# Two of eleven row-tile pairs in two feed-forward out projections computed as seven block products

## The chip, the cores and the metric

The kernel runs on one core of one Trainium2 chip. The metric is the device time of one execution in microseconds, the median of the runs. A profile comes from one execution more, whose own time is given beside it. Engines are named as in the profile: PE multiplies matrices, DVE and ACT and POOL work on tiles, SP issues the transfers.

## What is computed

A decoder trunk of two layers on 256 tokens of width 1024. Each layer wraps its mixer (a short gated convolution in the first layer, sparse attention in the second) in two half-step feed-forward blocks, so four such blocks run one after the other, each with an in projection (1024 to 5632) and an out projection (2816 to 1024). All data is float32.

```python
D_MODEL, SEQ, DEPTH, N_A_LAYERS, D_FF = 1024, 256, 2, 1, 2816

def swiglu_ffn(x, w_in, w_out):
    gate, up = jnp.split(x @ w_in, 2, axis=-1)
    return (jax.nn.silu(gate) * up) @ w_out

for i in range(DEPTH):
    if i == N_A_LAYERS:
        kv = shared_kv(h, ...)
    h = h + 0.5 * swiglu_ffn(rmsnorm(h, ffn1_norm[i]), ffn1_w_in[i], ffn1_w_out[i])
    hn = rmsnorm(h, mix_norm[i])
    if i < N_A_LAYERS:
        h = h + short_conv_mixer(hn, conv_w_in[i], conv_w[i], conv_w_out[i])
    else:
        h = h + nsa_mixer(hn, ...)
    h = h + 0.5 * swiglu_ffn(rmsnorm(h, ffn2_norm[i]), ffn2_w_in[i], ffn2_w_out[i])
```

The change concerns the two out projections of the first layer (i = 0): `ffn1_w_out[0]`, which stands before the convolution, and `ffn2_w_out[0]`, which stands before the shared K/V projection and the second layer.

## The kernel before

**Split products.** Every float32 operand is split in two fp32r tiles: `high`, a cast, and `low`, the float32 value less that cast. A product of two operands is the sum of high by high, high by low and low by high. An activation tile holds high and low side by side in 512 columns (256 tokens each). So one 128x128 block of weights against it takes two matmuls: the high weights against all 512 columns, the low weights against the first 256 (`half`).

**The stream of weights.** `Stream` (`W` in the code) brings the weights of the whole trunk in the order of use. SP loads 128x2048 pieces into three staging buffers `ws`. A unit is 1024 columns of one piece: ACT casts it into one of six `wh` buffers (`Stream.high`, L238), DVE subtracts into one of six `wl` buffers (`Stream.low`, L266). `W.take` hands a unit to PE's code, `W.done` frees it, and `W.pump` makes units as far ahead as free buffers allow. Program order is the order on each engine: an ACT or DVE instruction that waits holds up all that stands behind it there.

**In projection** (`ffn_in`). For each f of 22 (NF) tiles of 128 hidden rows, PE takes 32 matmuls of 512 columns' and 256 columns' kind, 16 each, into a pair of PSUM banks `mm` (two such pairs in turn). The evacuation of one f is: ACT copy (L448), DVE add (`total`, L449), DVE times the norm's factor R (L460), ACT Silu (L473), DVE product (L474), ACT cast (L442), DVE subtraction (L443), with the making of two units woven in between (`weave`, `ffn_evac`).

**Out projection** (`out_proj`). For each c of 8 (ND) tiles of 128 output rows, PE sums over the 22 hidden tiles k: 22 matmuls of 512 and 22 of 256 columns in one PSUM bank `a` (four in turn). `turn` alternates whether a c begins with its high or its low weights, so that two c's of the same kind meet. The weights lie c by c, so that one c uses 22 blocks, 2.75 units. `out_evac` adds the bank's two halves to the residual `h[c]` in two DVE instructions (L573) and then calls `Norm.tile(c)`: ACT (L379) and DVE (L383) make the next stage's split tile `xs[c]`, and POOL adds the squares (`Norm.squares`, L397, L398). After the last c POOL splits the sum of squares (L401, L402), and PE sums it over rows (`Norm.rows`, L408) inside the next stage's first group of matmuls, ahead of its last row tile. In the second of the two blocks `Norm.tile` makes two sets of tiles, one for the K/V projection and one for the second layer.

**Pairs.** The last block of the trunk (`ffn2_w_out[1]`, L1412) already has some row-tile pairs as seven block products, by class `Pairs`; the change doesn't touch what that block computes.

## Time and profile before

| what | value |
|---|---|
| time, median of 2 runs | 965.65 us (965.57 to 965.73) |
| profiled execution, its own time | 965.58 us |
| span of the profile | 963.8 us |
| work outside the span | 965.58 - 963.8 = 1.78 us |
| clock granted to PE | 1.00 |
| first out projection of layer 0, PE | 129.89 to 190.98 us from the span's start |
| second out projection of layer 0, PE | 402.74 to 463.83 us |

Times in the profile's rows are microseconds from the start of the span. A row of the timeline gives start, duration, engine, line, operation, output<-inputs, shapes and, in brackets, how long the engine had been idle and what ended that. Rows with xN merge N equal instructions; their duration is from the first start to the last end, so the step between starts is a little under duration / N.

### The profile page before, as it was taken

What the parts mean: (1) busy time and instruction counts of PE and PEld (TensorE: products, weight loads), DVE (VectorE), ACT (ScalarE), POOL (GpSimd) and SP (SyncE); (2) the same over time, 40 slices, a digit from 0 to 9 for tenths busy, and PEclk for the clock granted to TensorE, in tenths of its full rate; (3) what the DMA queues carried; (4) which work ended last, traced back from release to release, by engine and by line L of the source; (5) the groups of instructions that cost most, each with busy time, mean ns of one, the idle gap of its engine ahead of it and who ended that gap; (6) DMA issues with size and microseconds to landing.
All of it is one profiled execution on the core that took longest, in us unless ns stands there. A gap on an engine that the chain in (4) does not pass through costs nothing.

```text
span 963.8 us, 14683 instructions
## 1 busy us (share of the span) xinstructions
PE 958.1 (99%) x5609; PEld 839.4 (87%) x5609; DVE 755.0 (78%) x1213; ACT 581.9 (60%) x982; POOL 174.2 (18%) x266
## 2 busy tenths in 40 slices
PE   9999999999999999999999999999999999999998
PEld 7888888888888888888888888888987888888887
DVE  7987776678889888767659787866688788879896
ACT  7665653455556665644548787743479656656553
POOL 1000001144470100011321031001337350000002
PEclk9999999999999999999999999999999999999999
DMA  8665555546546975555635657554620364467362
GB/s 299 227 216 177 189 204 179 183 167 209 187 137 223 272 238 181 183 211 179 214 131 178 202 193 259 175 183 175 219 89 1 129 221 142 164 217 248 118 205 88
DMA packets 36423, 178.61 MB, mean 185 GB/s; under 512 B 3424, under 2 KB 7152, under 8 KB 18560
## 3 DMA queue, kind: packets, MB, share of 16 engines
q1 hardware_dynamic: 36352, 177.67, 54.1%
q8 instruction: 44, 0.72, 0.3%
q14 instruction: 27, 0.22, 0.1%
HBM read 175.52 MB, written 1.08 MB: 183 GB/s over the span
## 4 chain that ended last, share of the span: by engine, by line
PE 97%; DVE 1%; POOL 1%; DMA 0%; ACT 0%; issue 0%; SPq 0%; POOLq 0%
PE mm L430 55%; PE a L430 26%; PE a L1412 4%; PE mm L1412 2%; PE mm L1177 1%; PE a L1242 1%; PE a L812 1%; PE a L813 1%; PE a L814 1%; PE mm L655 1%; PE a L1222 1%; PE a L694 1%; DMA base<-in_first_dram 0%; POOL pr L1214 0%; DVE pr L1185 0%; PE a L925 0%
## 5 line engine op out<-in xcount | busy, mean ns | idle before, releaser
L266 DVE TENSOR_TENSOR wl<-ws,wh 128x1024 fp32r<-128x1024 f32 x263 | 326.5, 1252 | 68.4 <-ACT wh L238 42.8
L430 PE MATMUL mm<-xs,wh 128*128 128x512 f32 x1480 | 348.8, 390 | 0.0
L430 PEld LDWEIGHTS mm<-xs,wh 128*128 128x128 f32 x1480 | 273.6, 188 | 54.5 <-DVE xs L383 0.2
L238 ACT CAST wh<-ws 128x1024 fp32r<-128x1024 f32 x263 | 272.2, 1046 | 35.8 <-PE a L430 21.1
L430 PEld LDWEIGHTS mm<-xs,wl 128*128 128x128 f32 x1480 | 185.2, 192 | 4.2
L430 PE MATMUL mm<-xs,wl 128*128 128x256 f32 x1480 | 187.4, 283 | 0.0
L430 PE MATMUL a<-act,wh 128*128 128x512 f32 x608 | 141.7, 390 | 0.0
L430 PEld LDWEIGHTS a<-act,wh 128*128 128x128 f32 x608 | 113.0, 188 | 22.7
L449 DVE TENSOR_TENSOR t<-mm,t 128x512 f32<-128x512 f32 x95 | 65.2, 686 | 60.6 <-ACT t L448 59.9
L448 ACT COPY t<-mm 128x512 f32<-128x512 f32 x95 | 55.6, 585 | 73.7 <-PE mm L430 73.3
L430 PEld LDWEIGHTS a<-act,wl 128*128 128x128 f32 x608 | 75.7, 191 | 1.6
L430 PE MATMUL a<-act,wl 128*128 128x256 f32 x608 | 76.4, 283 | 0.0
L473 ACT ACTIVATE t<-t 128x256 f32<-128x256 f32 x88 | 36.8, 418 | 57.1 <-DVE t L460 57.0
L379 ACT ACTIVATE xs<-base 128x256 fp32r<-128x256 f32 x48 | 24.1, 506 | 77.0 <-DVE base L573 62.1
L460 DVE TENSOR_TENSOR t<-t,R 128x512 f32<-128x512 f32 (+1 forms) x88 | 57.3, 651 | 2.6
L442 ACT CAST act<-t 128x256 fp32r<-128x256 f32 x91 | 37.0, 407 | 28.8 <-DVE t L743 18.2
L397 POOL TENSOR_TENSOR t<-base 128x256 f32<-128x256 f32 x35 | 26.3, 751 | 134.7 <-DVE base L573 108.5
L443 DVE TENSOR_TENSOR act<-t,act 128x256 fp32r<-128x256 f32 x91 | 38.6, 424 | 5.7 <-ACT act L442 5.7
L383 DVE SCALAR_TENSOR_TENSOR xs<-base,xs 128x256 fp32r<-128x256 f32 x48 | 29.7, 622 | 16.9 <-ACT xs L379 16.8
L394 POOL TENSOR_TENSOR sq<-base 128x256 f32<-128x256 f32 x5 | 3.1, 615 | 219.4 <-DVE base L573 211.0
L474 DVE TENSOR_TENSOR t<-t,t 128x256 f32<-128x256 f32 x88 | 36.8, 418 | 4.6 <-ACT t L473 4.6
L1437 POOL TENSOR_TENSOR t<-t,base 128x512 f32<-128x512 f32 x4 | 5.9, 1478 | 163.6 <-ACT t L1435 163.6
(318 smaller groups left out, 1148.5 us busy)
## 6 DMA issues: line engine op xcount, KB each, us to landing
ws<-in_ffn_w_in_dram SPq DMA_DIRECT2D x69, 1024.0 KB, 5.0
ws<-in_ffn_w_out_dram SPq DMA_DIRECT2D x33, 1024.0 KB, 4.8
ws<-in_conv_w_in_dram SPq DMA_DIRECT2D x12, 1024.0 KB, 4.8
base<-in_ffn_w_in_dram SPq DMA_DIRECT2D x11, 1024.0 KB, 5.3
ws<-in_w_kv_dram SPq DMA_DIRECT2D x6, 1024.0 KB, 4.9
base<-in_ffn_w_pairs_dram SPq DMA_DIRECT2D x12, 512.0 KB, 4.7
kt<-in_ffn_w_in_dram SPq DMA_DIRECT2D x5, 1024.0 KB, 7.9
ws<-in_conv_w_out_dram SPq DMA_DIRECT2D x4, 1024.0 KB, 5.0
```

The lines of the kernel that those rows point to most:

```text
L238: ac.copy(h, src)
L266: ve.tensor_tensor(out=l, in0=src, in1=h.bitcast(F32), op=ALU.subtract)
L383: ve.scalar_tensor_tensor(out=xs[c][:, T:], in0=h[c], scalar=gt[:, g + c:g + c + 1], in1=xs[c][:, :T].bitcast(F32), op0=ALU.mult, op1=ALU. ...
L430: pe.matmul(o if x == 0 else o[:, :T], u[x][:, q * P:(q + 1) * P], rhs if x == 0 else rhs[:, :T], start=start, stop=stop, skip_group_check ...
L442: ac.copy(dst[:, :T], src)
L443: ve.tensor_tensor(out=dst[:, T:], in0=src, in1=dst[:, :T].bitcast(F32), op=ALU.subtract)
L448: ac.copy(r, o[:, :, T:])
L449: ve.tensor_tensor(out=r, in0=o[:, :, :T], in1=r, op=ALU.add)
L460: ve.tensor_tensor(out=r, in0=r, in1=R[:, None, :].to_broadcast([P, n, T]), op=ALU.mult)
L473: ac.activation(s, r[:, 0], AF.Silu)
L474: ve.tensor_tensor(out=s, in0=s, in1=r[:, 1], op=ALU.mult)
L1412: pe.matmul(m[n], x, w, start=(count[n] == 0 and i == 0), stop=(count[n] == total[n] - 1 and i == 2), skip_group_check=True)
```

## The change

Let X be the activations of two hidden row tiles (256 rows) against 256 tokens, seen as 2x2 blocks of 128x128, and W the matching 256x1024 weights, seen as 2x2 blocks of 128x512. The product is now formed from seven products of a 128x128 block of (sums of) X with a 128x512 block of (sums of) W, in place of eight. This is done for the pairs 4 and 5 of the eleven pairs (hidden tiles 8 to 11) in both out projections of layer 0. The other 18 hidden tiles stay as they were, and so does `ffn1_w_out[1]`, which goes through the new class with no pair chosen.

- **Weights** (`_blocks`, `add_out`, `four_high`, `sums`): the four blocks of a pair come as one 128x2048 piece. Its units ("kinds") are: 0, blocks 0 and 1; 1, block 3 alone (512 columns); then DVE forms four sums of blocks in place (`sums`, three instructions of 1024, 512 and 512 columns); 2 and 3, two sums each. Each kind is split in high and low as any unit. So a pair takes 3584 columns of splitting where its two row tiles took 2048.
- **Activations** (`Fours`, `factors`): as f = 8 to 11 are evacuated, three of the four X blocks and four sums of blocks are split, the sums in `pr` buffers.
- **Products** (`out_fours`): X is the stationary operand, W the moving one. Each product takes three matmuls of 512 columns (high high, low high, high low); products of the same number of both pairs are summed in one PSUM bank, seven banks in all. Between the two pairs, PE does the first eight row tiles of c = 0 (`ahead`).
- **Combining**: ACT copies one bank (L663), DVE adds the others in seven instructions (`plus`, L659) into four 128x512 tiles. These have tokens on partitions; DVE transposes them in 32x32 blocks (L677, four instructions), ACT moves 32-partition strips into place (`move`, L684, 16 instructions, issued two at a time as a unit is done with), and at c = 3 (`ADDED`) DVE adds four tiles to the residual (`add_fours`, L694).
- **Norm**: the `Norm.tile` calls of c = 0, 1, 2 wait until `add_fours` has run, so at c = 3 four of them stand in a row.

In the rows below, line numbers of the changed kernel are its own (L307 is `low`, L275 and L180 the casts, L199 `sums`, L698 `out_evac`, L424 and L420 the norm's tile). The number behind a tile tells tiles apart; `pr`, `wh`, `wl`, `ws`, `act`, `a`, `mm`, `kt` and `t` are the buffers' names.

PE at the start of the first out projection, before (the last rows of the first c's high weights, and the first of its low ones):

```order
L430 MATMUL a_1372<-act_1201,wh_1294 128x512
L430 MATMUL a_1372<-act_1254,wh_1294 128x512
L430 MATMUL a_1372<-act_1307,wh_1294 128x512
L430 MATMUL a_1372<-act_339,wl_1243 128x256
L430 MATMUL a_1372<-act_346,wl_1243 128x256
L430 MATMUL a_1372<-act_399,wl_1243 128x256
```

and now (the first pair's kinds 0 and 1, and half of kind 2):

```order
L647 MATMUL a_1394<-wh_1258,act_671 128x512 x2
L647 MATMUL a_1394<-wl_1260,act_671 128x512
L647 MATMUL a_1395<-wh_1258,act_724 128x512 x2
L647 MATMUL a_1395<-wl_1260,act_724 128x512
L647 MATMUL a_1396<-pr_1265,pr_732 128x512
L647 MATMUL a_1396<-pr_1265,pr_733 128x512
L647 MATMUL a_1396<-pr_1267,pr_732 128x512
L647 MATMUL mm_1398<-wh_1275,pr_732 128x512
L647 MATMUL mm_1398<-wh_1275,pr_733 128x512
L647 MATMUL mm_1398<-wl_1277,pr_732 128x512
```

What moved: the 32 matmuls per pair that had the weights as the stationary operand (16 of 512 and 16 of 256 columns, spread over all c's) became 21 of 512 columns, each kind taken once, at the head of the projection.

DVE from the end of the last f's evacuation, before (four of the units that the projection starts on, and the first c's end):

```order
L443 TENSOR_TENSOR act_1360<-t_230_1351,act_1360 128x256
L266 TENSOR_TENSOR wl_1404<-ws_1303,wh_1402 128x1024
L266 TENSOR_TENSOR wl_1418<-ws_1303,wh_1414 128x1024
L573 SCALAR_TENSOR_TENSOR base<-a_1372,base 128x256 x2
L383 SCALAR_TENSOR_TENSOR xs_1363<-base,xs_1363 128x256
L266 TENSOR_TENSOR wl_1459<-ws_1356,wh_1457 128x1024
L266 TENSOR_TENSOR wl_1473<-ws_1356,wh_1469 128x1024
L266 TENSOR_TENSOR wl_1485<-ws_1416,wh_1483 128x1024
```

and now:

```order
L199 TENSOR_TENSOR ws_1318<-ws_1318 128x1024
L199 TENSOR_TENSOR ws_1318<-ws_1318 128x512 x2
L307 TENSOR_TENSOR wl_1411<-ws_1318,wh_1409 128x1024
L307 TENSOR_TENSOR wl_1426<-ws_1318,wh_1422 128x1024
L307 TENSOR_TENSOR wl_1436<-ws_1327,wh_1434 128x1024
L307 TENSOR_TENSOR wl_1458<-ws_1327,wh_1454 128x1024
L659 SCALAR_TENSOR_TENSOR t_267_1483<-mm_1398,t_266_1481 128x512
L659 SCALAR_TENSOR_TENSOR t_266_1481<-a_1395,t_266_1481 128x512
L307 TENSOR_TENSOR wl_1488<-ws_1424,wh_1486 128x1024
L659 SCALAR_TENSOR_TENSOR t_270_1490<-mm_1399,t_267_1483 128x512
L659 SCALAR_TENSOR_TENSOR t_270_1490<-a_1396,t_270_1490 128x512
L307 TENSOR_TENSOR wl_1497<-ws_1424,wh_1493 128x1024
```

What moved: the block sums and four half-sized or whole units of the second pair stand ahead of the first ordinary units (wl_1436, wl_1458), and the adding of the products' banks (L659) stands between the next ones (wl_1488, wl_1497). The same subtractions for the first pair stand 15 rows earlier. PE's second c (a_1547) begins with low weights and reads wl_1497 in its fifteenth matmul.

ACT around the first c's of the projection, before:

```order
L379 ACTIVATE xs_1363<-base 128x256
L238 CAST wh_1457<-ws_1356 128x1024
L238 CAST wh_1469<-ws_1356 128x1024
L238 CAST wh_1483<-ws_1416 128x1024
L379 ACTIVATE xs_1364<-base 128x256
L238 CAST wh_1525<-ws_1416 128x1024
```

and now:

```order
L275 CAST wh_1572<-ws_1495 128x1024
L684 COPY t_283_1539<-kt_1513 32x512 x2
L275 CAST wh_1588<-ws_1509 128x1024
L684 COPY t_290_1592<-kt_1513 32x512 x2
L275 CAST wh_1624<-ws_1509 128x1024
L684 COPY t_290_1592<-kt_1513 32x512 x2
L275 CAST wh_1640<-ws_1574 128x1024
L684 COPY t_297_1644<-kt_1513 32x512 x2
L275 CAST wh_1676<-ws_1574 128x1024
L684 COPY t_297_1644<-kt_1513 32x512 x2
L275 CAST wh_1692<-ws_1626 128x1024
L684 COPY t_304_1696<-kt_1513 32x512 x4
```

What moved: 16 moves, all of which read the transposed tile kt_1513, stand between the casts of the units for the fourth to sixth c; the norm's tiles (L379, now L420) of the first c's stand behind them.

The diff, cut to what the prediction speaks of:

```diff
+FOURS = {"ffn1": ((4, 5), ()), "ffn2": ((4, 5), ())}
+ADDED = 3
...
+        def add_fours(self, src, spare):
+
+            for kind in range(4):
+                if spare and kind == 1:
+                    self.spare.add(len(self.where))
+                self.where.append((len(self.src), kind, "four"))
+            self.src.append(src)
+
+        def add_out(self, four, rest):
+
+            self.add_fours(four[:, :CHUNK], True)
+            self.add(rest, 0, 1024)
+            self.add_fours(four[:, CHUNK:], False)
+            self.add(rest, 1024)
...
+        def four(self, tag, i, n):
+            if i in self.spare:
+                return mk([P, 1, 512], "pr", 6, F32R)
+            return mk([P, 2, 512], tag, NBUF, F32R)[:, :n]
+
+        def four_high(self, st, kind):
+            if kind == 2:
+                while self.half:
+                    self.low()
+                self.sums(st)
+            src = st[:, 3:] if kind == 1 else st[:, 2:] if kind == 2 else st[:, :2]
+            h = self.four("wh", len(self.units) + len(self.half), src.shape[1])
+            ac.copy(h, src)
+            self.half.append((src, h))
...
+    class Fours(Pairs):
+
+
+        late = False
+
+        def __init__(self, pairs):
+            super().__init__(lambda n: [mk([P, 512], "pr", 6, F32R) for _ in range(2)])
+            self.pairs, self.rest = pairs, []
+
+        def add(self, s):
+            self.f.append(s)
+            p, odd = divmod(len(self.f) - 1, 2)
+            if p in self.pairs:
+                self.factors(s, odd)
+                return
+            hd = act()
+            split(s, hd)
+            self.rest.append(hd)
...
+    RIGHT = {1: (0, 1), 2: (0, 0), 3: (1, 0), 4: (3, 0), 5: (3, 1), 6: (2, 1), 7: (2, 0)}
+
+    def out_fours(hid, factor):
+
+
+        m = {n: bank() for n in (1, 2, 3)}
+        ahead, t67, t45 = bank(), bank2(), bank2()
+        m[6], m[7], m[4], m[5] = t67[:, 0], t67[:, 1], t45[:, 0], t45[:, 1]
+        last = len(hid.left) - 1
+        for p, left in enumerate(hid.left):
+            for ns in (1, 2), (3,), (6, 7), (4, 5):
+                u, = W.take()
+                for n in ns:
+                    (xh, xl), (kind, at) = left[n - 1], RIGHT[n]
+                    wh, wl = [t[:, at] for t in u]
+                    for i, (x, w) in enumerate(((xh, wh), (xl, wh), (xh, wl))):
+                        pe.matmul(m[n], x, w, start=(p == 0 and i == 0), stop=(p == last and i == 2))
+                W.done(1, p < last)
+            if p == 0:
+                u, = W.take()
+                for x in (0, 1):
+                    for k in range(8):
+                        half(ahead, u, x, k, hid.rest[k], x == 0 and k == 0, False)
+                turn[0] = 1
+                W.done(1)
+                Y["head"] = ahead
+
+        def plus(o, n, base):
+            ve.scalar_tensor_tensor(out=o, in0=m[n], scalar=factor, in1=base, op0=ALU.mult, op1=ALU.add)
+            return o
+
+        s1 = t2()
+        ac.activation(s1, m[1], AF.Copy, scale=factor)
+        u = plus(t2(), 6, s1)
+        plus(s1, 2, s1)
+        yield
+        c12 = plus(t2(), 5, u)
+        plus(c12, 3, c12)
+        yield
+        plus(u, 7, u)
+        c22 = plus(t2(), 5, u)
+        yield
+        plus(u, 4, u)
+        yield
+        Y["turned"] = mk([P, 4, 512], "kt", 1)
+        for tt, x, t in ((0, 0, s1), (0, 1, c12), (1, 1, c22), (1, 0, u)):
+            ve.transpose(Y["turned"].rearrange("p a (t x c m) -> p t x a c m", t=2, x=2, c=4)[:, tt, x].rearrange("p a c m -> p c a m"),
+                         t.rearrange("p (c a m) -> p c a m", c=4, a=4))
+            yield
+
+        def move(b, a):
+            if a == 0:
+                Y[b] = t2()
+            ac.copy(Y[b][32 * a:32 * a + 32], Y["turned"][32 * b:32 * b + 32, a])
+
+        Y["moves"] = [lambda b=b, a=a: move(b, a) for b in range(4) for a in range(4)]
+
+    def add_fours():
+        for go in Y.pop("moves"):
+            go()
+        del Y["turned"]
+        for b in range(4):
+            v = kt8[:, :, :T].rearrange("p c (t b m) -> p b t c m", t=2, b=4)[:, b]
+            ve.tensor_tensor(out=v, in0=Y[b].rearrange("p (t c m) -> p t c m", t=2, c=ND), in1=v, op=ALU.add)
 
     def out_evac(o, c, factor, norm, prep=True):
         for x in range(2):
             ve.scalar_tensor_tensor(out=h[c], in0=o[:, x * T:(x + 1) * T], scalar=factor, in1=h[c], op0=ALU.mult, op1=ALU.add)
         if prep and c < ND - 1:
             W.low()
-        norm.tile(c)
+        if "turned" in Y and c < ADDED:
+            pass
+        elif "turned" in Y:
+            add_fours()
+            for k in range(c + 1):
+                norm.tile(k)
+        else:
+            norm.tile(c)
         if prep:
             if c == ND - 1:
                 W.low()
             W.high()
 
-    def out_proj(lhs, factor, norm, final=False):
-
+    def out_proj(lhs, factor, norm):
+
+        if isinstance(lhs, Fours):
+            if lhs.left:
+                weave(out_fours(lhs, factor), 5)
+            lhs = lhs.rest
         n, i, u = len(lhs), 0, None
         head = []
         if n == 8:
@@ -591,37 +727,30 @@
             a_pass([(o, u, lhs, [7])])
             W.done(1, False)
             out_evac(o, c, factor, norm)
-        for c in range(len(head), ND - final):
-            o = bank()
-            run = []
-            for k in range(n):
+        for c in range(len(head), ND):
+            o = Y.pop("head", None)
+            k0 = 0 if o is None else 8
+            o = bank() if o is None else o
+            run = [None] * k0
+            i += k0
+            for k in range(k0, n):
                 if i % 8 == 0:
                     u, = W.take()
                 run.append((u, i % 8, i % 8 == 7))
                 i += 1
             first = n - (c == 0 and n != 8)
-            for ks in (range(first), range(first, n)):
+            for ks in (range(k0, first), range(first, n)):
                 ways = (turn[0], 1 - turn[0]) if ks else ()
                 for m, x in enumerate(ways):
                     for k in ks:
                         half(o, run[k][0], x, run[k][1], lhs[k], m == 0 and k == 0, m == 1 and k == n - 1)
                         if m == 1 and run[k][2]:
                             W.done(1, k < n - 1)
+                            for go in Y.get("moves", ())[:2]:
+                                go()
+                                Y["moves"].remove(go)
...
```

More of the change, by code (lines that the diff above doesn't have):

```diff
@@ L217, in high @@
             st = self.stage[c]
+            if joint == "four":
+                self.four_high(st.rearrange("p (a n) -> p a n", n=512), u)
+                if u == 3:
+                    self.load(c + 2)
+                return
             src = st[:, 2 * u:2 * u + 2] if c in self.other else st[:, u * 1024:min((u + 1) * 1024, self.src[c].shape[1])]
@@ L262, in low @@
                 return
-            l = mk([P, 1024], "wl", NBUF, F32R)
-            if len(src.shape) == 3:
-                l = l.rearrange("p (a n) -> p a n", n=512)
+            four = self.where[len(self.units)][2] == "four"
+            if four:
+                l = self.four("wl", len(self.units), src.shape[1])
+            else:
+                l = mk([P, 1024], "wl", NBUF, F32R)
+                if len(src.shape) == 3:
+                    l = l.rearrange("p (a n) -> p a n", n=512)
             ve.tensor_tensor(out=l, in0=src, in1=h.bitcast(F32), op=ALU.subtract)
-            if len(src.shape) == 3:
+            if len(src.shape) == 3 and not four:
                 h, l = [t.rearrange("p a n -> p (a n)") for t in (h, l)]
@@ L293, in trunk @@
     W.add(A["ffn1_w_in"][0])
-    W.add(A["ffn1_w_out"][0])
+    W.add_out(A["ffn1_w_four0"], A["ffn1_w_out0"])
     W.add(A["conv_w_in"])
@@ L297, in trunk @@
     W.add(A["ffn2_w_in"][0])
-    W.add(A["ffn2_w_out"][0])
+    W.add_out(A["ffn2_w_four0"], A["ffn2_w_out0"])
     W.add(A["w_kv"])
@@ L304, in trunk @@
     W.add(A["ffn1_w_in"][1], (W1AT[1] + 1) * 2048)
-    W.add(A["ffn1_w_out"][1])
+    W.add(A["ffn1_w_out1"])
     W.add(A["attn_w_q"], 0, 2048)
@@ L309, in trunk @@
     W.add(A["attn_w_o"])
-    W.spare = set(range(len(W.where) - 2, len(W.where) + 1))
+    W.spare |= set(range(len(W.where) - 2, len(W.where) + 1))
     W.add(A["ffn2_w_in"][1])
@@ L468, in ffn_evac @@
     def ffn_evac(r, R, hid):
-        late = isinstance(hid, Pairs)
+        late = hid.late
         times(r[:, :2 - late], R, 2 - late)
@@ L475, in ffn_evac @@
         yield
-        if late:
-            hid.add(s)
-            return
-        hd = act()
-        split(s, hd)
-        hid.append(hd)
+        hid.add(s)
     class Pairs:
+        late = True
         def __init__(self, homes):
@@ L543, in ffn_in @@
     def ffn_in(xs, norm, R=None, bg=None, pre=None, sums=(), rms=None, hid=None):
-        hid, sums = [] if hid is None else hid, list(sums)
+        sums = list(sums)
         box = [R]
@@ L609, in out_proj @@
                             W.done(1, k < n - 1)
+                            for go in Y.get("moves", ())[:2]:
+                                go()
+                                Y["moves"].remove(go)
                 turn[0] = ways[1] if ks else turn[0]
             out_evac(o, c, factor, norm, n != 8 or c not in (5, 6))
-        if final:
-            us = W.take((i + n + 7) // 8 - i // 8 - (i % 8 > 0))
-            us = ([u] if i % 8 else []) + us
-            w = [[us[(i % 8 + k) // 8][x][:, (i + k) % 8 * P:((i + k) % 8 + 1) * P] for x in range(2)] for k in range(n)]
-            o, last = bank(), bank()[:, :T]
-            for k in range(n):
-                pe.matmul(o, w[k][0], lhs[k], start=(k == 0), stop=(k == n - 1))
-            for k in range(n):
-                pe.matmul(last, w[k][1], lhs[k][:, :T], start=(k == 0), stop=(k == n - 1))
-            for part in (o[:, :T], o[:, T:], last):
-                ve.scalar_tensor_tensor(out=h[c + 1], in0=part, scalar=factor, in1=h[c + 1], op0=ALU.mult, op1=ALU.add)
-            norm.tile(c + 1)
         W.pump(1 if n == 8 else NBUF)
@@ L718, in first_rms @@
         return r
-    hid = ffn_in(xs, nm, sums=first_tiles(), rms=first_rms)
+    hid = ffn_in(xs, nm, sums=first_tiles(), rms=first_rms, hid=Fours(FOURS["ffn1"][0]))
     xs = new_xs()
@@ L1484, in _rows, with _blocks @@
     return w.reshape(k, 128, m, 128).transpose(1, 2, 0, 3).reshape(128, -1)
+def _blocks(w):
+    w = w.reshape(-1, 2, 128, 2, 512)
+    return np.concatenate([w[:, 1, :, 0], w[:, 0, :, 0], w[:, 0, :, 1], w[:, 1, :, 1]], 2).transpose(1, 0, 2).reshape(128, -1)
 def _layout(i):
@@ L1493, in _layout @@
         r[n + "_w_in"] = w.reshape(2, 8, 128, 2, NF, 128).transpose(0, 2, 4, 3, 1, 5).reshape(2, 128, -1)
-        r[n + "_w_out"] = np.stack([_rows(w) for w in a[n + "_w_out"]])
-    r["ffn2_w_out"] = r["ffn2_w_out"][:1]
-    w = a["ffn2_w_out"][1].reshape(NF // 2, 2, 128, 2, 512)
-    r["ffn2_w_pairs"] = np.concatenate([w[:, 1, :, 0], w[:, 0, :, 0], w[:, 0, :, 1], w[:, 1, :, 1]], 2).transpose(1, 0, 2).reshape(128, -1)
+        w = a[n + "_w_out"].reshape(2, NF // 2, 2, 128, D)
+        for l in range(3 - int(n[3])):
+            q = FOURS[n][l]
+            r[f"{n}_w_out{l}"] = _rows(np.delete(w[l], q, 0).reshape(-1, D))
+            if q:
+                r[f"{n}_w_four{l}"] = _blocks(w[l][list(q)])
+    r["ffn2_w_pairs"] = _blocks(a["ffn2_w_out"][1].reshape(NF // 2, 2, 128, D))
     w = r["ffn1_w_in"][0][:, :4096].reshape(128, 2, 2, 8, 128).transpose(0, 3, 1, 2, 4).reshape(128, 8, 512)
```

20 lines of the change are left out of this document (12 added, 8 removed).

## The prediction

> **What bounds the kernel now.** I read the busy times first, then the chain of waits, then the list of waits for PE, and at last the timeline of the first changed out projection.
>
> ```profile
> span 963.8 us, 14683 instructions
> PE 958.1 (99%) x5609; PEld 839.4 (87%) x5609; DVE 755.0 (78%) x1213; ACT 581.9 (60%) x982; POOL 174.2 (18%) x266
> PE 97%; DVE 1%; POOL 1%; DMA 0%; ACT 0%; issue 0%; SPq 0%; POOLq 0%
> ...
> PE a L348 <- DVE ones L328: 1.1, 1, 1.1
> ...
> PE a L1222 <- POOL pr L1214: 0.2, 1, 0.2
> ```
>
> PE is busy throughout, and the chain that ends last runs through PE alone. Of PE's waits the list has four groups, the first and the last shown, all small. So time is what PE issues, plus any new wait on it. The other engines cost nothing as long as PE never waits for them; whether they have room is read from the stage.
>
> ```profile
> start us, us, engine line op out<-in xcount [idle before <-releaser]
> 129.89 4.92 PE L430 MATMUL a<-act,wh 128*128 128x512 f32 x21
> ...
> 147.80 10.16 PE L430 MATMUL a<-act,wh 128*128 128x512 f32 x44
> 157.80 5.43 PE L430 MATMUL a<-act,wl 128*128 128x256 f32 x44
> 163.07 10.16 PE L430 MATMUL a<-act,wh 128*128 128x512 f32 x44
> ...
> 190.98 2.91 PE L430 MATMUL mm<-xs,wh 128*128 128x512 f32 x12
> ...
> 130.00:191.00 61.00, 61.00 (x354) 54.05 (x353) 37.55 (x48) 27.69 (x33) 9.27 (x13) 1.00 0.54 190
> ```
>
> The projection lasts from 129.89 to 190.98. 44 matmuls of 512 columns take 157.80 - 147.80 = 10.00 us, 0.2273 each; 44 of 256 take 5.27 us, 0.1198 each; both of a block 0.3471. In the last row the columns after the span of the stretch are PE, PEld, DVE, ACT and POOL: DVE is busy for 37.55 of 61 us, ACT for 27.69.
>
> **What PE saves.** The moving operand is now the weights. The K/V projection already runs so:
>
> ```profile
> 469.30 0.39 PE L812 MATMUL a<-wh,t 128*128 128x512 f32 x1
> ...
> 471.34 0.39 PE L812 MATMUL a<-wh,t 128*128 128x512 f32 x1
> ```
>
> Nine matmuls from one row to the other take 2.04 us, 0.227 each, the same pace. Per projection the four row tiles leave, 32 blocks x 0.3471 = 11.11 us, and 42 x 0.2273 = 9.55 us come. The saving is 1.56 us, in two projections 3.1 us. Nothing else leaves PE.
>
> **What DVE gets ahead of the second c.** The rows that price it, one f's evacuation, block sums as the last block of the trunk has them, lows, and an add out of PSUM:
>
> ```profile
> 119.60 0.69 DVE L449 TENSOR_TENSOR t<-mm,t 128x512 f32<-128x512 f32 x1 [1.18 <-ACT t L448]
> ...
> 125.14 0.69 DVE L449 TENSOR_TENSOR t<-mm,t 128x512 f32<-128x512 f32 x1 [1.13 <-ACT t L448]
> 125.86 0.69 DVE L460 TENSOR_TENSOR t<-t,R 128x512 f32<-128x512 f32 x1
> 126.47 1.22 DVE L266 TENSOR_TENSOR wl<-ws,wh 128x1024 fp32r<-128x1024 f32 x1
> 127.61 0.42 DVE L474 TENSOR_TENSOR t<-t,t 128x256 f32<-128x256 f32 x1
> 127.98 1.23 DVE L266 TENSOR_TENSOR wl<-ws,wh 128x1024 fp32r<-128x1024 f32 x1
> 129.12 0.42 DVE L443 TENSOR_TENSOR act<-t,act 128x256 fp32r<-128x256 f32 x1
> ...
> 173.57 3.50 DVE L266 TENSOR_TENSOR wl<-ws,wh 128x1024 fp32r<-128x1024 f32 x3 [2.44 <-PE a L430]
> ...
> 914.38 2.67 DVE L167 TENSOR_TENSOR base<-base 128x1024 f32<-128x1024 f32 x3
> 916.43 2.00 ACT L161 CAST wh<-base 128x1024 fp32r<-128x1024 f32 x2 [4.06 <-DVE base L167]
> 917.52 1.23 DVE L172 TENSOR_TENSOR wl<-base,wh 128x1024 fp32r<-128x1024 f32 x1 [0.47 <-ACT wh L161]
> ...
> L172 DVE TENSOR_TENSOR xs<-base,xs 128x512 fp32r<-128x512 f32 x3 | 2.0, 683 | 0.0
> L1429 DVE SCALAR_TENSOR_TENSOR t<-mm,t 128x512 f32<-128x512 f32 x2 | 1.4, 687 | 0.8 <-ACT t L1435 0.8
> ```
>
> An f costs DVE 4.40 us (125.14 to 129.54), and PE gives it a new one after 125.14 - 119.60 = 5.54; that slack is all it has. From 119.60 (f = 19) DVE's queue up to the low of wl_1497 holds: f = 19 with one 512-column low, 3.87 (a whole low steps by 1.14, a half one by some 0.61); block sums 2.6 (2.67 as a row; the next work overlaps a little) and the wait for the cast of their result 0.47; its low 1.18; f = 20, 4.40; f = 21, again with a half low, 3.87; sums and wait, 3.07; four lows 4.65 (three take 3.50); then four adds at 0.72 and two lows, 5.25. Together 29.4 us: wl_1497 is there at 149.0. I take the adds a little above their row's 0.687, since each second one reads what the one before it wrote.
>
> PE wants it at 129.89 + 9.55 + 16 matmuls of the unit between the pairs 2.78 + the ten other blocks of c = 0, 3.47 + fourteen low matmuls of c = 1, 1.68 = 147.4. So PE waits 1.6 us, whether there or in pieces before. That eats the saving in each projection.
>
> Edits that I cost at nothing. The split of the X blocks and their sums at f = 9 and 11 is at most 0.61 + 4 x 0.42 = 2.3 us more on DVE, in an f that has 1.1 to spare; the next f and the second `mm` pair take the rest, and without them PE would wait 1.2 us. Transfers:
>
> ```profile
> ws<-in_ffn_w_out_dram SPq DMA_DIRECT2D x33, 1024.0 KB, 4.8
> ```
>
> SP's queue gets two more of them for the same bytes. The tightest is the piece for c = 2, issued when kind 3 of the second pair is split, near 141.5 by the tally, landed at 146.3, wanted by PE at 153.5; were those 7 us gone, PE would wait for each microsecond beyond.
>
> **What ACT and the norm get behind it.** From 149.0 DVE needs three adds 2.1, two lows 2.3 and four transposes to let ACT move.
>
> ```profile
> L1378 DVE STREAM_TRANSPOSE t<-base 128x512 f32<-128x512 f32 x4 | 2.8, 706 | 0.0
> 139.82 3.09 ACT L238 CAST wh<-ws 128x1024 fp32r<-128x1024 f32 x3
> L161 ACT CAST xs<-base 128x512 fp32r<-128x512 f32 x3 | 1.8, 614 | 0.0
> L907 ACT COPY wh<-act 64x240 f32<-64x240 f32 x8 | 3.1, 390 | 0.1
> ...
> 191.60 0.88 DVE L573 SCALAR_TENSOR_TENSOR base<-a,base 128x256 f32<-128x256 f32 x2
> 193.06 0.48 DVE L383 SCALAR_TENSOR_TENSOR xs<-base,xs 128x256 fp32r<-128x256 f32 x1 [0.58 <-ACT xs L379]
> 195.56 0.74 POOL L402 TENSOR_TENSOR t<-sq,t 128x256 fp32r<-128x256 f32 x1
> 198.30 0.40 PE L408 MATMUL a<-t,ones 128*128 128x256 f32 x2
> ```
>
> A strided 32x32 transpose has no row; the plain one takes 0.706 and I take that (bounds 0.7 to 1.4, were the scattered output half as fast). They end at 156.2. A 32-partition copy has none either: bounds 0.39 (64 partitions, 240 columns) and 0.61 (512 columns, 128 partitions). I take 0.57, near the second, since it has the column count. 16 moves and six casts at 1.0 end at 171.3. Then on DVE come c = 3's evacuation, four residual adds at 0.69, and four norm tiles in step with ACT, to 176.4; three lows behind a cast, and c = 4's evacuation starts at 180.8. PE (with its 1.6 us) has ended c = 4 at 172.3: DVE is 8.5 us late. Units stay ahead (the cast for c = 6 is wanted at 179.4, there at 177.2). Each later c costs DVE 0.88 + 0.58 + 0.48 + 0.45 for a cast + 2.33 for two lows = 4.7 of PE's 6.25, so at c = 7 it is 3.9 late, against 191.60 - 190.98 = 0.62 before. The sum of squares is ready 196.30 - 190.98 = 5.3 after PE's end and used 7.3 after; that slack of 2.0 is overrun by 1.3. In the second projection two sets of norm tiles make four norm tiles eight (1.7 more) and each c 5.2; the last unit of c = 7 is then 0.4 late, while the K/V stage wants the last tile some 9 us after PE's end and waits for nothing.
>
> By the Trainium skill, "ScalarE: Activation LUTs", section "What ACT_TABLE_LOAD costs", an instruction with immediate operands takes 186 ns + 0.833 ns per column, whatever its partitions: that speaks against the 16 strips, 0.613 us each. No run here shows a 32-partition copy; by it the moves end 0.7 us later, and the sum is at most 2 x 0.7 more, 968.8.
>
> **Sum.** -3.1 + 2 x 1.6 + 1.3 + 0.4 = +1.8 us on the profiled execution's 965.58 (span 963.8 and 1.78 around it): 967.4. That execution lies 0.07 under the median of 965.65.
>
> **Rivals.**
> *No new wait.* DVE's adds and sums overlap better than I priced, 1.6 us in 29 decide it, and the norm catches up. For it: 1.1 us of DVE idling in each f. Time: 965.6 - 3.1 = 962.5. Chance 0.25.
>
> *POOL and DVE slow each other.* After c = 3 POOL squares four tiles in a row, seven instructions, beside DVE.
>
> ```profile
> 206.46 1.23 DVE L266 TENSOR_TENSOR wl<-ws,wh 128x1024 fp32r<-128x1024 f32 x1
> ...
> 209.93 1.65 DVE L266 TENSOR_TENSOR wl<-ws,wh 128x1024 fp32r<-128x1024 f32 x1 [0.26 <-ACT wh L238]
> ...
> 210.57 1.51 POOL L731 TENSOR_TENSOR u<-u,R 128x256 f32<-128x256 f32 x1
> ```
>
> A low beside a POOL product takes 0.42 more. Seven times that is 2.9 us on an already late DVE, in both projections: 967.4 + 5.8 = 973.2 at most, half of it 970.3. Against it: the norm's row at 193.06 stands beside POOL's squares and keeps its 0.48. Chance 0.22. The Trainium skill, "GPSIMD Engine Reference", section "1. Specifications", says that POOL's SBUF interfaces are shared with DVE's where DVE has two SBUF inputs; the trace agrees (1.65 against 1.23).
>
> *Slow moves*, the one on the other side. The unit for c = 5 is there at 169.2 and wanted at 173.0, behind twelve moves: above 0.57 + 0.32 = 0.9 us each PE begins to wait, and the residual adds and norm come later with them. At 1.2 us the moves end 16 x 0.63 = 10 us later, and PE waits about as long in each projection, 967.4 + 20 = 987. For it: no row shows the shape; against it, the 64-partition copy's 0.39. Chance 0.05.
>
> **Chances.** The forecast has 0.48 (own range 965 to 969). Range 962.5 to 972: its ends are the first rival and most of the second; about 0.1 lies outside. A change of 2% is 19.3 us, about what a measurement of this kernel can tell from no change; the saving can't reach it, slow moves above 1.2 us could: 0.01 faster, 0.97 same, 0.02 slower.
>
> **What would show it.** Right: PE waits of 1 to 2 us for `wl` between 138 and 150, and about 1 us for `Norm.rows` near 199; DVE without idling from 123 to 150; the moves near 0.57. Wrong: no wait for `wl` in the first two c's (DVE's price too high); moves or transposes off their rows; a wait at c = 5 or 6 that I don't have; any wait inside the in projection.

## The result and the profile after

| | before | after |
|---|---|---|
| time, median | 965.65 us (2 runs) | 971.4 us (2 runs, 971.13 to 971.67) |
| ratio to before | | 1.0057, 95% interval 1.0041 to 1.0074 |
| span of the profile | 963.8 us | 969.3 us |
| DVE busy | 755.0 us, 78% | 799.1 us, 82% |
| clock granted to PE | 1.00 | 1.00 |

The changed kernel is 0.6% slower, and the interval lies clear of 1 (the prediction took 2% for about the least that can be told from no change; the interval here is 0.3% wide). It is within the 2% that counts as the same. It is 4.0 us above the predicted 967.4: inside the range of 962.5 to 972, but outside 965 to 969, the range of the forecast by itself.

PE's first matmul of each part gives the parts' lengths in the two traces. The parts are the first out projection, from there to the second one (norm, convolution, feed-forward in projection), the second out projection, and the K/V projection.

| part | before | after | difference | predicted |
|---|---|---|---|---|
| start of the first projection | 129.89 | 130.09 | +0.20 | 0 |
| first projection | 61.09 | 60.85 | -0.24 | -1.56 + 1.6 = 0.0 |
| to the second projection | 211.76 | 214.37 | +2.61 | +1.3 |
| second projection | 61.09 | 62.72 | +1.63 | -1.56 + 1.6 + 0.4 = +0.4 |
| K/V projection | 22.29 | 23.60 | +1.31 | 0 |
| all after it | 477.68 | 477.67 | 0.0 | 0 |

The differences add up to 5.5 us, the difference of the spans. So the loss lies in three places, each at the end of a projection or just behind it, and none in the long stages between. The list of PE's waits in the changed kernel names them (engine, line, what was waited for: us in all, how often, the longest):

```profile
PE a L471 <- DVE wl L307: 2.7, 3, 1.8
PE a L449 <- POOL t L442: 1.7, 1, 1.7
PE a L941 <- ACT sm L462: 1.0, 1, 1.0
PE a L449 <- POOL t L443: 0.4, 1, 0.4
```

The first row is two waits of 0.47 in the heads of the projections (their start, up to the second c) and one of 1.8 for the last low of c = 7 in the second projection; the second and fourth are the row sums of the first norm; the third is the K/V projection, which waits for its own norm's square root. In the chain of work that ended last, PE has 84% of the span and DVE and ACT have 8% and 4%.

The new operations, each by its row, in the groups of instructions (mean ns of one behind the bar's first number) and the timeline of the changed kernel:

```profile
L684 ACT COPY t<-kt 32x512 f32<-32x512 f32 x32 | 19.8, 618 | 10.5 <-DVE kt L677 10.0
L677 DVE STREAM_TRANSPOSE kt<-t 128x512 f32<-128x512 f32 x8 | 5.0, 679 | 0.0
L694 DVE TENSOR_TENSOR base<-t,base 128x512 f32<-128x512 f32 x8 | 5.0, 687 | 0.1
```

A move takes 0.62 us (0.57 taken), a strided transpose 0.68 (0.706 taken), an add 0.69. In the head, the low that PE's second c waits for is done at 148.5 (149.0 predicted), and PE goes on at 148.60:

```profile
148.60 0.74 PE L471 MATMUL a<-act,wl 128*128 128x256 f32 x4 [0.47 <-DVE wl L307]
```

So far the tally holds. It ceases to hold behind the residual adds, on DVE and POOL at c = 3 of the first projection, where the four norm tiles stand in a row (below: the batch):

```profile
169.26 1.23 DVE L307 TENSOR_TENSOR wl<-ws,wh 128x1024 fp32r<-128x1024 f32 x1 [1.12 <-ACT wh L275]
...
171.31 2.50 DVE L694 TENSOR_TENSOR base<-t,base 128x512 f32<-128x512 f32 x4
...
174.39 2.88 DVE L424 SCALAR_TENSOR_TENSOR xs<-base,xs 128x256 fp32r<-128x256 f32 x4 [0.58 <-ACT xs L420]
...
177.06 0.80 POOL L439 TENSOR_TENSOR sq<-sq,t 128x256 f32<-128x256 f32 x1
177.19 4.99 DVE L307 TENSOR_TENSOR wl<-ws,wh 128x1024 fp32r<-128x1024 f32 x3
177.83 1.59 POOL L438 TENSOR_TENSOR t<-base 128x256 f32<-128x256 f32 x1
...
179.50 1.60 POOL L439 TENSOR_TENSOR sq<-sq,t 128x256 f32<-128x256 f32 x1
182.10 0.87 DVE L698 SCALAR_TENSOR_TENSOR base<-a,base 128x256 f32<-128x256 f32 x2
...
183.55 0.49 DVE L424 SCALAR_TENSOR_TENSOR xs<-base,xs 128x256 fp32r<-128x256 f32 x1 [0.58 <-ACT xs L420]
183.80 0.84 POOL L439 TENSOR_TENSOR sq<-sq,t 128x256 f32<-128x256 f32 x1
```

Three lows take 4.99 us, where three alone take 3.50, and the four norm tiles 2.88. POOL's squares run beside them and are slowed themselves, from 0.80 to 1.60. Beside these lows the two engines end in turn: the lows at 178.95, 180.50 and 182.18, the squares at 179.42 and 181.10. That looks as if each waited for the other, but no run tests it. The evacuation of c = 4 starts at 182.10; the prediction had 180.8.

### The profile page after: what moved, and what is told of

It is laid out like the page before. It is cut to its first block, busy times and chain, and to the rows that moved or that the text cites. A ratio compares the mean times of both kernels' runs of the same rounds, so it can differ in the third digit from the quotient of the medians.

```text
span 969.3 us, 14725 instructions
## 1 busy us (share of the span) xinstructions
PE 957.2 (99%) x5565; PEld 835.3 (86%) x5565; DVE 799.1 (82%) x1283; ACT 609.3 (63%) x1028; POOL 179.2 (18%) x266
## 4 chain that ended last, share of the span: by engine, by line
PE 84%; DVE 8%; ACT 4%; issue 3%; DMA 1%; POOL 0%; SPq 0%; ACTq 0%; DVEq 0%
PE mm L471 54%; PE a L471 14%; PE a L1541 4%; DVE wl L307 3%; ACT wh L275 2%; PE mm L1541 2%; ACT t L684 1%; PE mm L1306 1%; PE mm L647 1%; PE a L647 1%; PE a L1371 1%; DVE base L698 1%; DVE t L659 1%; PE a L1351 1%; DMA base<-in_first_dram 1%
## 5 line engine op out<-in xcount | busy, mean ns | idle before, releaser
L307 DVE TENSOR_TENSOR wl<-ws,wh 128x1024 fp32r<-128x1024 f32 (+1 forms) x269 | 334.7, 1256 | 46.2 <-ACT wh L275 37.2
L275 ACT CAST wh<-ws 128x1024 fp32r<-128x1024 f32 x255 | 263.4, 1046 | 23.6 <-PE a L471 7.3
L471 PE MATMUL a<-act,wh 128*128 128x512 f32 x544 | 127.6, 390 | 0.0
L471 PEld LDWEIGHTS a<-act,wh 128*128 128x128 f32 x544 | 100.8, 188 | 20.1
L471 PEld LDWEIGHTS a<-act,wl 128*128 128x128 f32 x544 | 68.5, 191 | 5.4 <-DVE wl L307 3.3
L471 PE MATMUL a<-act,wl 128*128 128x256 f32 x544 | 70.2, 284 | 2.7 <-DVE wl L307 2.7
L420 ACT ACTIVATE xs<-base 128x256 fp32r<-128x256 f32 x48 | 23.8, 506 | 64.7 <-DVE base L698 47.3
L424 DVE SCALAR_TENSOR_TENSOR xs<-base,xs 128x256 fp32r<-128x256 f32 x48 | 29.9, 631 | 15.5 <-ACT xs L420 15.4
L438 POOL TENSOR_TENSOR t<-base 128x256 f32<-128x256 f32 x35 | 28.3, 808 | 74.6 <-DVE base L698 68.3
```

The costliest lines, as they stand in the source:

```text
L275: ac.copy(h, src)
L307: ve.tensor_tensor(out=l, in0=src, in1=h.bitcast(F32), op=ALU.subtract)
L424: ve.scalar_tensor_tensor(out=xs[c][:, T:], in0=h[c], scalar=gt[:, g + c:g + c + 1], in1=xs[c][:, :T].bitcast(F32), op0=ALU.mult, op1=ALU. ...
L471: pe.matmul(o if x == 0 else o[:, :T], u[x][:, q * P:(q + 1) * P], rhs if x == 0 else rhs[:, :T], start=start, stop=stop, skip_group_check ...
```

## Experiments

Part lengths below are taken as in the table above.

**1. No pair, or pairs in one projection only.** The table of chosen pairs is emptied, for both or for one of the projections (the weights then come as one whole again).

```diff
-FOURS = {"ffn1": ((4, 5), ()), "ffn2": ((4, 5), ())}
+FOURS = {"ffn1": ((), ()), "ffn2": ((), ())}
```

> No pair is chosen in either projection, all else is the changed kernel. Every theory expects the time of the kernel before, 965.6 us within 1 us. Were it 968 or more, the cost would lie in code beside the products (another order of banks or units), and all theories on waits behind the products would fall.

> Only the first projection has the seven products. Late-tail theory (the changed profile's milestones: -0.2 in the projection, +2.6 at the norm's row sums): 968.0 us, and no wait in the second. Head theory (DVE's sums and adds cost what is lost, in both projections alike): half of +5.7, 968.5. The two differ in where PE waits: at the row sums near 200 us (late tail), or at a low before 150 us (head).

> Only the second projection has them. Late-tail theory: +1.6 in the projection (a wait of 1.8 us for the last low of c = 7) and +1.3 in the K/V stage, together 968.5 us. If the two projections' losses were not independent (one taking over lateness from the other), only1 and only2 would not add up to the +5.7 us of both.

Without pairs the time is 965.86 us (ratio 1.0002, 0.9993 to 1.0011): nothing else in the new code costs time that can be told from none. Pairs in the first projection alone give 969.52 (1.0039, 1.0024 to 1.0053), in the second alone 969.01 (1.0036, 1.0023 to 1.0049). The parts of the second kernel repeat those of the full change (62.74 and 23.59 us against 62.72 and 23.60): each projection does its damage by itself. The first kernel waits at the row sums (1.67 and 0.42 us) and only 0.4 in the head, as the late-tail theory has it. Over the 965.79 us of the kernel before in these runs the two are 3.7 and 3.2 us, which add up to 6.9 and not to the 5.7 of both together; the first of them, 1.5 us above the late-tail theory's 968.0, has an extra loss that the section on the hardware shows.

**2. Without the squares in the batch.**

```diff
             for k in range(c + 1):
-                norm.tile(k)
+                norm.tile(k, k == 0)
```

> Leaves out POOL's squares of the row tiles 1 to 3 in the batch at c = 3 (so the sum of squares misses them); DVE and ACT work as before. Contention theory (POOL and DVE slow each other in the batch, some 2.7 us of DVE in each projection): the lows behind the batch take 3.5 instead of 5.0 us, the wait at the row sums falls from 2.6 to below 1, the one for c = 7's low from 1.8 to below 0.5; time 967.5 to 968.5. Rival (DVE is late by its own work and by ACT's moves): under 0.7 us less, 970.7 or more.

968.01 us (1.0021, 1.0010 to 1.0032), 3.4 us under the changed kernel. The same stretch of its timeline:

```profile
174.52 1.69 DVE L424 SCALAR_TENSOR_TENSOR xs<-base,xs 128x256 fp32r<-128x256 f32 x4 [0.58 <-ACT xs L420]
...
176.66 3.50 DVE L307 TENSOR_TENSOR wl<-ws,wh 128x1024 fp32r<-128x1024 f32 x3 [0.46 <-ACT wh L275]
...
180.07 0.88 DVE L698 SCALAR_TENSOR_TENSOR base<-a,base 128x256 f32<-128x256 f32 x2
```

The norm tiles go from 2.88 to 1.69, the lows from 4.99 to 3.50: 2.7 us of DVE's time, of which 2.0 arrive at c = 4, since DVE now waits 0.46 for a cast. The same six products of POOL are all that was taken away. The wait for the last low of c = 7 is gone (second projection 60.79 us, 1.93 less), and 1.62 of the 2.61 us before the second projection. The K/V projection stays at 23.56 (the section on the prediction shows why).

**3. The norm tiles dealt out.**

```diff
             add_fours()
-            for k in range(c + 1):
-                norm.tile(k)
+            Y["late"] = list(range(c + 1))
+            for _ in range(2):
+                norm.tile(Y["late"].pop(0))
+        elif Y.get("late"):
+            Y["late"].append(c)
+            for _ in range(min(2, len(Y["late"]))):
+                norm.tile(Y["late"].pop(0))
```

> The changed kernel with the four norm tiles that follow the residual adds dealt out over c = 3, 4 and 5, two at each, instead of four in a row at c = 3. All work stays. Theory (POOL's squares in a row slow DVE beside them): the squares still come beside DVE's lows, but in pairs; each pair costs less waiting in the queue at c = 3, the same work is only moved to c = 4 and 5, so c = 4's evacuation starts about 2 us sooner than in the changed kernel (about 180.1 instead of 182.1) and c = 7's by at most 1 us: 970 to 971.4. Rival (only the standing in a row is the harm, and two at a time run free as in the kernel before): POOL's products keep their 0.61 to 0.84, DVE's lows 1.23, and the time comes to that of the kernel without the squares, 968.0.

969.71 us (1.0042, 1.0026 to 1.0058), 0.3 below the theory's range and 1.7 above the rival's value. The evacuation of c = 4 starts at 180.64, but POOL's products still stretch the work beside them:

```profile
175.90 4.82 DVE L307 TENSOR_TENSOR wl<-ws,wh 128x1024 fp32r<-128x1024 f32 x3
...
181.42 1.61 DVE L424 SCALAR_TENSOR_TENSOR xs<-base,xs 128x256 fp32r<-128x256 f32 x2
182.96 2.90 DVE L307 TENSOR_TENSOR wl<-ws,wh 128x1024 fp32r<-128x1024 f32 x2
```

Dealing moves the contention and takes only a part of it away.

**4. Units made ahead of the sums of the products.**

```diff
+        yield
+        yield
         s1 = t2()
         ac.activation(s1, m[1], AF.Copy, scale=factor)
```

> The changed kernel with two units of weights made (cast and low) ahead of the sums of the block products instead of between and behind them. If DVE's queue at the start of the projection is the cause of PE's waits for wl there, these waits (0.9 us in all in the trace of the changed kernel's first projection and some in the second) go, about 1.3 us a projection. If DVE is one queue from there to c = 7 whose total decides, the sums, transposes and moves come 2.4 us later, the batch at c = 3 too, and the row sums and the last low of c = 7 give back 1 to 2 us each: 970.5 to 972.5, the same within a microsecond. Rival (the two ends are not coupled, since ACT's moves leave slack): 968.8 to 969.2.

972.7 us (1.0070, 1.0054 to 1.0086), 0.2 above the theory's range. The waits in the head are gone, but the first projection is no shorter (61.15 us): PE waits for the last low of c = 7 in both projections, 0.91 us in the first, where there was no such wait, and 2.60 in the second.

```profile
186.33 1.22 PE L471 MATMUL a<-act,wl 128*128 128x256 f32 x8 [0.91 <-DVE wl L307]
...
463.72 2.07 PE L471 MATMUL a<-act,wl 128*128 128x256 f32 x8 [2.60 <-DVE wl L307]
465.59 6.29 PE L471 MATMUL a<-act,wh 128*128 128x512 f32 x18
```

So what PE gains at its start it loses at its end, as the theory has it. The theory's size is off: DVE begins c = 4's evacuation at 182.66, only 0.56 later and not 2.4, and PE's wait for the row sums stays at 1.6. That the time is above the changed kernel's isn't all DVE's doing: in the last two rows above PE's matmuls run slow behind the wait (last section), which costs some 2.9 us in this profile (2.07 and 6.29 us, where 1.21 and 4.27 are usual).

**5. Without the moves.** The adds read the transposed tile, first with the adds at c = 1, then with the adds and the batch of four left at c = 3.

```diff
-            if a == 0:
-                Y[b] = t2()
-            ac.copy(Y[b][32 * a:32 * a + 32], Y["turned"][32 * b:32 * b + 32, a])
+            Y[b] = Y["turned"][:, b]
```

> Leaves out the sixteen moves on ACT (the adds read the transposed tile where it stands, so the sums go to other rows), and does the residual adds at c = 1 instead of c = 3, so that two norm tiles and not four stand in a row. Theory (what is late at the end of the projection is the batch at c = 3, which the moves force there): no wait for the row sums beyond 0.4, none for the last low of c = 7 in the second projection, K/V stage's wait for its own row sums gone; left are the waits at the head, 1.3 a projection: 965.65 - 3.1 + 2.6 + 0 to 1 = 965 to 966.2. Rival (DVE's own load of sums, transposes and adds, about 9 us more in each projection, is what makes the tail late, wherever the adds stand): 968 to 970.

> Leaves out the sixteen moves on ACT (the adds read the transposed tile where it stands, so the sums go to other rows) and keeps the adds and the batch of four norm tiles at c = 3: the other half of the experiment in which the adds also came at c = 1 (965.03). If the moves are harmful because DVE's lows wait for casts that stand behind them on ACT (0.49 + 1.12 + 0.33 + 1.12 + 0.33 + 1.12 = 4.5 us of idle DVE between 157 and 170 in the changed kernel's first projection), the evacuation of c = 3 and the adds start 3 to 4.5 us sooner (170.40 before them), the batch still costs its 2.1 us of contention, c = 4's evacuation starts near 178, and the time is 965.5 to 967. If the place and size of the batch alone are the harm, nothing is won by taking away the moves: 970 to 971.5.

965.03 us (0.9992, 0.9982 to 1.0002) with the adds at c = 1, and 965.41 (0.9996, 0.9987 to 1.0005), 0.1 below its range, with the adds at c = 3: the place of the batch hardly counts once the moves are gone. So the first theory's number came true, but not for its reason, the batch at c = 3. The second kernel's timeline:

```profile
160.07 2.35 DVE L307 TENSOR_TENSOR wl<-ws,wh 128x1024 fp32r<-128x1024 f32 x2
...
167.34 2.50 DVE L691 TENSOR_TENSOR base<-kt,base 128x512 f32<-128x512 f32 x4
...
170.42 2.88 DVE L424 SCALAR_TENSOR_TENSOR xs<-base,xs 128x256 fp32r<-128x256 f32 x4 [0.58 <-ACT xs L420]
...
173.22 4.99 DVE L307 TENSOR_TENSOR wl<-ws,wh 128x1024 fp32r<-128x1024 f32 x3
...
178.13 0.87 DVE L696 SCALAR_TENSOR_TENSOR base<-a,base 128x256 f32<-128x256 f32 x2
```

The batch costs DVE the same 2.88 and 4.99 us, yet it costs PE nothing: it comes 4.0 us sooner (adds at 167.34, not 171.31), because two lows follow each other in 2.35 us, and DVE doesn't stand idle for casts that wait behind a pair of moves on ACT: between 157 and 170 it waits 0.84 us for casts, and 4.5 in the changed kernel. All waits at the ends of the projections, the K/V projection's too (22.27 us), are gone. What is left is the head: the projections take 60.68 and 60.69 us, 0.4 less than before and not 1.56.

**6. The moves on another engine.** As transfers on SP's queue behind the transposes, with the adds at c = 1; or half of them on POOL, with the adds at c = 2 or 3, and in two of the three kernels the tiles dealt out as in 3.

```diff
-            ac.copy(Y[b][32 * a:32 * a + 32], Y["turned"][32 * b:32 * b + 32, a])
+            sy.dma_start(Y[b][32 * a:32 * a + 32], Y["turned"][32 * b:32 * b + 32, a])
```

```diff
-            ac.copy(Y[b][32 * a:32 * a + 32], Y["turned"][32 * b:32 * b + 32, a])
+            to, of = Y[b][32 * a:32 * a + 32], Y["turned"][32 * b:32 * b + 32, a]
+            if b < 2:
+                ac.copy(to, of)
+            else:
+                po.tensor_copy(out=to, in_=of)
```

> The whole computation again: the sixteen moves as transfers on SP's queue right behind the transposes instead of copies on ACT, and the residual adds at c = 1 instead of c = 3. If the transfers land within some 5 us and take no room from the weights behind them on SP's queue, this comes to the time of the kernel without moves, 965 to 966.2 by the batch theory. Rival: the sixteen transfers stand ahead of the weights in SP's queue and wait there for the transposes; weights then land up to 5 us late, PE waits for wl at c = 1 to 3, and the time is 970 or above.

> The whole computation: eight of the sixteen moves (those of blocks 2 and 3) go to POOL, right behind the transposes, the other eight stay on ACT, and the residual adds come at c = 2 with a batch of three norm tiles instead of at c = 3 with four. In the trace of the changed kernel a pair of ACT moves and a cast take 2.30 us together, and DVE's lows wait for the casts (1.12 at every second one); half of these pairs go, so the moves end near 163.5 instead of 171.75. Theory (the moves on ACT and the batch that they force to c = 3 make the end of the projection late): c = 4's evacuation starts by 180.0, c = 7's by 193.5, no wait for the last low of c = 7 in the second projection, row-sum wait under 0.5, and the time is 965.5 to 967, if POOL's copies don't slow DVE's lows. Rival (POOL's eight copies slow the lows beside them by 0.42 each, as its products do, and what ACT gives is lost there): 968.5 to 971.

> The kernel with half the moves on POOL and the adds at c = 2, and besides the norm tiles dealt out, two at c = 2 and two at c = 3, instead of three at c = 2. The dealing took 1.7 us off the changed kernel's time (969.7 against 971.4), 1.5 us of it in the start of c = 4's evacuation. If the batch's contention still counts with three tiles (five products of POOL), this is 0.3 to 1 us under the kernel without the dealing; if the batch has slack at c = 2, the two are equal.

> The whole computation: half the moves on POOL, the norm tiles dealt out two at each c, and the residual adds at c = 3 again, where more units stand ready than at c = 2. In the kernel with the adds at c = 2 PE waited 2.8 us in all for lows behind the batch; here these waits should go, and the row sums should wait less than in the changed kernel with the dealing alone (0.7 and 0.4), since ACT's half of the moves ends 8 us sooner and DVE idles some 2 us less. Expected 966 to 968; if 965.5 or less, it beats both kernels. Rival (DVE's total work decides, wherever it stands, and POOL's copies slow it as much as ACT's queue did): 969 to 970, as with the dealing alone.

| moves | adds | tiles | time, us | ratio to before, interval |
|---|---|---|---|---|
| SP's queue | c = 1 | two in a row | 974.29 | 1.0087, 1.0071 to 1.0103 |
| ACT and POOL | c = 2 | three in a row | 970.49 | 1.0050, 1.0037 to 1.0062 |
| ACT and POOL | c = 2 | dealt out | 967.65 | 1.0022, 1.0013 to 1.0031 |
| ACT and POOL | c = 3 | dealt out | 966.15 | 1.0004, 0.9995 to 1.0013 |

The transfers met the rival: SP is held by them from 154.98 on, the next weights are issued at 165.53, and PE waits 2.0 us for a cast.

```profile
154.98 10.44 SPq L684 DMA_DIRECT2D t<-kt  x16
...
165.53 5.96 SPq L229 DMA_DIRECT2D ws<-in_ffn_w_out_dram  x3
...
169.58 2.99 PE L471 MATMUL a<-act,wh 128*128 128x512 f32 x7 [2.01 <-ACT wh L275]
```

The time of the kernel with the adds at c = 2, 970.49, lies in its rival's range, but the rival's reason is only a part of it. The lows beside POOL's copies lose 0.33, 0.20 and 0.05 us, less than the 0.42 that the rival reckoned with. The adds start at 167.24, as wanted, but the lows behind the batch come too late, and PE waits for them in the middle of both projections, a wait that neither theory had (the last row is of the second projection):

```profile
155.91 8.69 POOL L688 COPY t<-kt 32x512 f32<-32x512 f32 x8 [135.71 <-DVE kt L677]
...
174.05 1.22 PE L471 MATMUL a<-act,wl 128*128 128x256 f32 x8 [0.55 <-DVE wl L307]
...
450.10 2.35 PE L471 MATMUL a<-act,wl 128*128 128x256 f32 x12 [2.35 <-DVE wl L307]
```

Dealing the tiles out took 2.8 us off there, more than expected; about 1.1 of it may be PE's clock, which fell behind the 2.35 us wait (36 matmuls in 9.43 us, where 8.35 is usual). The last kernel came out inside its range: 5.2 us under the changed kernel, and the same as the kernel before. Its parts are 60.67, 211.86, 60.70 and 23.47: the losses behind both projections are gone but for the K/V projection's 1.2, and this and the two heads use up the saving. It doesn't beat the kernel before.

## Why the prediction was right, and where it was short

- **PE's saving: right.** The first pair's 21 matmuls and the unit behind it took 4.76 and 2.77 us in the trace (130.09 to 134.85 and 137.62), as priced.
- **The head (1.6 us in each projection): right in kind, a little large.** The first projection is 0.24 shorter, so 1.56 - 0.24 = 1.3 us of the saving are lost in it; without the squares or without the moves 1.56 - 0.41 = 1.15 are, so nearly all of it is the head's. One listed wait of 0.47 and small gaps ahead of it, in the second pair and in the lows of the second c, make up most of it.
- **The term that failed: the stretch behind the moves, priced as if POOL were not there.** The prediction wrote "four norm tiles in step with ACT, to 176.4; three lows behind a cast, and c = 4's evacuation starts at 180.8", on the ground that the norm's row at 193.06 stands beside POOL's squares and keeps its 0.48. The reading of that row was right, and the rows at 183.55 and 183.80 show the same, but one tile doesn't tell of four. A single tile's squares fall mostly into DVE's waits around it, and even the part beside it doesn't slow it; why not is not shown. In the batch POOL has work without a break: the first tile still takes 0.48, the next three 0.84, 0.96 and 0.83, and tiles and lows together lose 2.7 us (the rival priced 2.9). The evacuation came at 182.10, 1.3 late, and no later c made it good: at c = 7 DVE stood 5.2 us behind PE, where the forecast had 3.9 and the kernel without the squares 3.6. Experiment 2 shows the share: 3.4 us of the time. The rival "POOL and DVE slow each other", given 0.22, is what happened on top of the forecast's own waits; its times, 970.3 to 973.2, hold the result. The result lies inside the stated range because this rival's lower times were taken into it, not because the forecast's sum held.
- **The norm's row sums (1.3 us): 2.6.** 1.6 of it is the contention. Without the squares 1.0 is left, near what the forecast had from the moves and adds alone.
- **The last low of c = 7 in the second projection (0.4 us): 1.8**, and nothing of it without the squares.
- **"The K/V stage ... waits for nothing": wrong, 1.3 us.** The forecast looked at when the last tile is wanted, not at what the norm's square root stands behind on ACT. The rows of the changed kernel:

```profile
474.93 0.51 ACT L420 ACTIVATE t<-base 128x256 fp32r<-128x256 f32 x1 [2.27 <-DVE base L698]
475.34 0.49 ACT L420 ACTIVATE xs<-base 128x256 fp32r<-128x256 f32 x1
...
475.74 3.89 ACT L275 CAST wh<-ws 128x1024 fp32r<-128x1024 f32 x4
...
479.65 1.28 ACT L462 ACT_TABLE_LOAD   x1
...
480.95 0.26 ACT L462 ACTIVATE sm<-a,epst 128x2 f32<-128x2 f32 x1
...
481.26 0.50 PE L941 MATMUL a<-wh,kt 128*128 128x512 f32 x1 [1.01 <-ACT sm L462]
```

  The last tile waits for DVE and holds ACT's queue, four casts stand behind it, and the table load and square root come after all four. So what counts is when the last tile starts on ACT after PE's first matmul of the stage: here 6.9 us after it, with a wait of 1.0. By that it is wanted about 6.9 - 1.0 = 5.9 after it, and not the forecast's 9. Without the moves it starts at 4.9, also ahead of four casts, and the wait is gone. Without the squares DVE is earlier, but PE reaches the stage as much earlier, the tile again starts at 6.9, and 1.0 us stays. An order with the square root ahead of the casts was not tried.
- **The moves (0.57 each): 0.62**, 0.8 us more in 16, and done at 171.75 where the tally had 171.3. A 32-partition move takes as long as the 128-partition row of as many columns (0.61). The rival "slow moves" did not come about. But they hurt in the way that the forecast's tally had it: experiment 5 shows that what was lost behind the projections goes with them. That experiment takes them away altogether; that it is their place ahead of the casts, and not only their time on ACT, is read from DVE's waits for casts there (0.84 us against 4.5).

Put together: without contention the parts are -0.43, +0.99, -0.30 and +1.27, a sum of +1.5 against the forecast's +1.8. That it is so near is in part chance, since a smaller head and the missed K/V wait cancel. The contention adds 3.4 us to the time, but only on top of the lateness from the moves: without them it costs PE nothing (experiment 5).

## What to carry to other kernels

When work is put off and then done in a row, the helpers that ran in the gaps of the single steps (here POOL's squares) run beside the main engine, and both must be priced at the contended rate. Lateness of an engine costs by whether the slack up to the next reader holds: here DVE began c = 4's evacuation 9.9 us after PE had ended that c (182.10 and 172.20), and PE waited later on; without the moves it began 5.9 after (178.13 and 172.21), and the same contention was free. Copies put between casts on an in-order engine cost twice here, once by their time, and once by the idle time of the engine that waits for the casts.

## What the hardware showed besides

**Behind a short wait PE's clock can fall to half.** In the kernel with pairs in the first projection alone, PE waits 1.67 us for the row sums, as in the changed kernel (1.66), but there the matmuls behind it run slower. Windows of its trace (stretch, length, busy time of PE, PEld, DVE, ACT and POOL with instructions, granted clock, DMA share, GB/s):

```profile
199.00:201.00 2.00, 0.38 (x1) 0.19 (x1) 1.05 (x1) 1.09 (x1) 1.89 (x2) 1.00 0.24 98
201.00:203.00 2.00, 1.83 (x9) 1.60 (x10) 0.90 (x1) 0.91 (x2) 0.11 (x1) 0.83 0.95 283
203.00:205.00 2.00, 2.00 (x6) 1.61 (x5) 2.00 (x3) 2.00 (x4) 1.07 (x3) 0.50 0.60 250
205.00:207.00 2.00, 2.00 (x8) 1.56 (x8) 2.00 (x3) 0.32 (x1) 1.92 (x2) 0.82 0.00 0
```

The granted clock falls to 0.50 for some 3 us, and the part up to the second projection is 216.00 us long, 1.6 more than in the changed kernel. That accounts for this kernel's 1.5 us above its expectation: of its four runs the one whose mean clock was 1.00 took 968.20 us, and the three at 0.997 or 0.998 took 969.46 to 970.12. After the 2.60 us wait of experiment 4 the same is seen (18 matmuls in 6.29 us, where they take 4.27), and in experiment 6 after waits of 2.01 (the row at 169.58) and 2.35. After the two longest waits of the changed kernel (1.66 and 1.77) the clock stayed at 1.00, and so it did after one of 2.53 in the kernel with the moves on SP's queue. So the length of the wait alone doesn't decide it. The Trainium skill, "TensorE: Matmul & The Clock Gate", section "What's actually happening", tells of a gate that halves the array's clock by its activity in free-running windows of about 3.4 us. Windows that run free would fit that one wait has the effect and another of its length, or a longer one, has not; but the page names an idle window of about 3.4 us as what brings the fall, and these waits are shorter. No run here settles that.

**POOL as a copier.** A 32x512 copy takes POOL 8.69 / 8 = 1.09 us and ACT 0.62, and in the kernel of that row (experiment 6) lows beside POOL's copies take 1.56, 1.43 and 1.28 us instead of 1.23: here a copy with one input slowed DVE too.
